# The softmax's division on ScalarE, and other PSUM banks for the first key and value projection, in a hybrid attention and DeltaNet layer

## The chip, the cores and the metric

One NeuronCore of one Trainium2 chip runs the whole kernel. The metric is the device time of one execution in microseconds (us), lower is better. The engines are TensorE (PE; its weight loads are listed apart as PEld), VectorE (DVE), ScalarE (ACT), GpSimd (POOL) and SyncE (SP, which issues most of the loads). Each engine takes its instructions from its own queue in order, so an instruction that waits holds up all that stand behind it in that queue.

## What is computed

One decoder layer, 1024 positions, width 1024, float32:

```
u   = RMSNorm(x);  proj = u @ w_in      # [attn q | k | v | dn q | dn k | dn v | dn z | dn b | dn a]
A   = sliding-window attention (128), 8 query heads, 2 key/value heads, rotary, a sink per head:
        probs = softmax(concat([q k^T * scale + mask, sink]))[..., :-1];  A = probs @ v
B   = gated DeltaNet, 4 heads of 128: conv4 + SiLU, l2 norm, beta, decay, chunks of 64:
        T = (I + L)^-1 per chunk, then a scan over chunks, gated RMSNorm
h   = x + concat(A, B) @ w_o
h  += relu(RMSNorm(h) @ w_up)^2 @ w_down
h  += sigmoid(RMSNorm(h) @ w_gate) * (p @ w_proj);   out = RMSNorm(h)
```

The part that is changed is `probs`: the exponentials of a block of scores, divided by their sum. The other part, the projection `u @ w_in` for the columns of k, v, b and a of the first 512 positions, computes what it did.

## The kernel before

**Matmuls.** Every float32 operand of a projection is split in two fp32r parts, hi and lo, and each product is three passes (hi·hi, hi·lo, lo·hi; `mm3`). A weight slice comes by a load of SyncE into one of two buffers `raw`; ScalarE copies it to hi (L219), VectorE or GpSimd subtracts to get lo (L220), and the pair `w` has four buffers.

**Order.** Generators (`prepare`, `chain`, `attend`, `pairs`, with `projections` as filler) issue the work in a rough interleaving; then the scheduler of the tile framework orders each engine's queue by its own model of durations and readiness. So an edit of one helper moves instructions of other helpers, on every engine, from the edited place until the layer's up projection.

**PSUM.** Eight banks in three rings: g has 3 (the projections), d has 4 (the attention, and the first inverse), e has 1 (small matmuls). `gemm_a` takes its four banks by a string of ring names. The first query projection takes "gggd"; so does the first key/value projection behind it (`CKV`, 96 matmuls of 128x264, weight slices w25, w27, w31 and w35), so that in the kernel before its banks are those that the query projection has to give back by four copies (L478). Its results leave by twelve ScalarE instructions (`kv_evac`, L470 to L472), once the rows' norms are there (`prepare`: `u_rstd`, then `rows_rstd`, which builds `dg` on VectorE and `rsb0` from a matmul over it). The decay scalars (`scalars`, L629 to L652, ending in `gg`) start from `ba`, the last of these results. The first DeltaNet key projection (`CDK`, weight slices w40, w49, w57, w59) follows.

**Attention.** 32 units, each two heads by one block of 128 queries. A unit: four score matmuls into a d bank, masked maximum on VectorE (L549), exponential with its sum on ScalarE, a head at a time (L555), reciprocal of the sums on VectorE (L557), the product of both heads with it (L558), four transposes of `s` on TensorE (L106), a copy to `pt` (L569, VectorE or ScalarE by turns), and the product with v. `s` has three buffers. A unit is two steps behind its scores (`lag`). Filler matmuls of the projections stand between a unit's steps on TensorE.

**DeltaNet.** Per half of 512 positions: convolution (`conv_evac`, L404 to L415), l2 norms, `pre`, an inverse of 31 steps on VectorE alone (L773 to L778), four merges (L800 to L830), then a scan of four pairs of chunks in two head groups (L885 to L958). Filler between these is what is left of `projections`, the embedding product and the output projection `w_out`. The up and down projections and the gate follow.

Of the kernel before, what the change touches and what calls it, by code (L numbers as in the profile page):

```python
# [12 lines left out]
AF = mybir.ActivationFunctionType  # L13
ALU = mybir.AluOpType
# [15 lines left out]
CQ, CKV, CDQ, CDK, CDV, CDZ = 0, 512, 776, 1288, 1800, 2312  # L30
NKV = 264
# [20 lines left out]
class Flow:  # L52
# [11 lines left out]
    def step(self):  # L64
        for x in self.tasks:
            w = x[1]
            if w.done if isinstance(w, (Event, Banks)) else w <= self.now:
                try:
                    w = next(x[0])
                    x[1] = w if isinstance(w, (Event, Banks)) else self.now + w  # L70
                except StopIteration:
                    self.tasks.remove(x)
                return
        if self.filler and (self.hold is None or self.hold.done):
            try:
                self.hold = next(self.filler)
            except StopIteration:
                self.filler = None
            return
        if self.spare:  # L80
            try:
                next(self.spare)
            except StopIteration:
                self.spare = None
            return
        self.now = min(x[1] for x in self.tasks if not isinstance(x[1], (Event, Banks)))
# [23 lines left out]
def bc(ap, dim, n):  # L110

    a = ap.unsqueeze(dim)
    shape = list(a.shape)
    shape[dim] = n
    return a.to_broadcast(shape)
# [3 lines left out]
def hybrid_block(ctx, tc, t, out):  # L119
    nc = tc.nc  # L120
    V, A, G, SY = nc.vector, nc.scalar, nc.gpsimd, nc.sync
# [4 lines left out]
    def nm(s):  # L126
        cnt[0] += 1
        return f"{s}{cnt[0]}"
# [28 lines left out]
    def take(k):  # L157

        live = ring[k]
        while live.n == 0:  # L160
            yield live
        live.n -= 1
        b = bank(ps[k])

        def free():
            live.n += 1
        return b, free
# [54 lines left out]
    def wunit(src, n=512, lo_eng=None, sp=None, raw=None):  # L222
        if raw is None:
            raw = wraw.tile([P, WN], F32, tag="raw", name=nm("raw"))
        SY.dma_start(raw[:, :n], src)
        w = (sp or wsp).tile([P, 2, 512 if sp else WN], F32R, tag="w", name=nm("w"))
        split(w[:, 0, :n], w[:, 1, :n], raw[:, :n], lo_eng or G)
        return w[:, :, :n]
# [3 lines left out]
    def mm3(o, lh, rh, first, last, **k):  # L232
        for i, (a, b) in enumerate(PASSES):
            T.matmul(o, lh(a), rh(b), start=first and i == 0, stop=last and i == 2, **k)
# [9 lines left out]
    def uview(u, b, kt):  # L244
        o = (b * KT + kt) * HB
        return u[:, o:o + HB]

    def gemm_a(c0, u, evac, names, n=512, lo_eng=None, step=None, done=None, after=None, raws=None):

        bs = []  # L250
        for k in names:
            bs.append((yield from take(k)))
        for kt in range(KT):
            if step:
                step(kt)
            if 2 * n > WN:
                w, o = wunit(t["w_in"][kt * P:(kt + 1) * P, c0:c0 + n], n, lo_eng, raw=raws and raws(kt)), 0
            elif kt % 2 == 0:
                w, o = wunit2(t["w_in"], kt // 2, c0, lo_eng, n), 0
            else:  # L260
                o = n
            for m in range(4):
                mm3(bs[m][0][:, :n], lambda a: uview(u, a, kt)[:, m * P:(m + 1) * P],
                    lambda b: w[:, b, o:o + n], kt == 0, kt == KT - 1)
                yield
        if done:
            done.done = True
        if after:
            yield after
        for m in range(4):  # L270
            evac(m, bs[m][0])
            bs[m][1]()
# [121 lines left out]
    def rs(tt):  # L394
        return rstd[:, tt:tt + 1]
# [47 lines left out]
    U0 = up0.__enter__().tile([P, 8192], F32R, tag="U0", name="U0")  # L443
# [22 lines left out]
    def kv_evac(hb):  # L466
        def evac(m, b):
            tt = hb * 4 + m
            kraw[tt] = scr[:, 1024 + m * P:1024 + (m + 1) * P]
            A.activation(kraw[tt], b[:, 0:P], AF.Copy, scale=rs(tt))  # L470
            A.activation(vA[:, tt], b[:, P:2 * P], AF.Copy, scale=rs(tt))
            A.activation(ba[:, tt], b[:, 2 * P:NKV], AF.Copy, scale=rs(tt))  # L472
        return evac
# [59 lines left out]
    def att_scores(n, gp, kv, qT):  # L533

        lo = 0 if n else P
        h0 = kv * 4 + gp * 2
        st = lambda x: atp.tile([P, 2], F32, tag=x, name=nm(x), bufs=4)
        b, free = yield from take("d")
        mx, sm = st("mx"), st("sm")
        s = atp.tile([P, 2, 257], F32, tag="s", name=nm("s"), bufs=3)  # L540
        G.tensor_copy(s[:, :, 256], sinkB[:, h0:h0 + 2])
        b = b.rearrange("p (g s) -> p g s", g=2)
        j = slice(n % 4 + lo // P, n % 4 + 2)
        for i in range(2):
            o = b[:, i, lo:256].rearrange("p (j s) -> p j s", s=P)
            T.matmul(o, qT[:, kv, gp * 2 + i], kH[:, kv, j], start=True, stop=False)
            T.matmul(o, qT[:, kv, gp * 2 + i], kL[:, kv, j], start=False, stop=True)
        for i in range(2):
            V.tensor_tensor_reduce(  # L549
                out=s[:, i, lo:256], in0=b[:, i, lo:256], in1=amask[:, lo:256],  # L550
                scale=1.0, scalar=NEG, op0=ALU.add, op1=ALU.max, accum_out=mx[:, i:i + 1])
        free()
        V.scalar_tensor_tensor(mx, mx, -1.0, nsink[:, h0:h0 + 2], op0=ALU.mult, op1=ALU.min)  # L553
        for i in range(2):
            A.activation(s[:, i, lo:257], s[:, i, lo:257], AF.Exp, bias=mx[:, i:i + 1],  # L555
                         accum_out=sm[:, i:i + 1])
        V.reciprocal(sm, sm)  # L557
        V.tensor_tensor(s[:, :, lo:256], s[:, :, lo:256], bc(sm, 2, 256 - lo), op=ALU.mult)  # L558
        return s

    def att_pt(n, kv, s):
# [521 lines left out]
    def projections():  # L1083
        yield from gemm_a(CQ, U0, lambda m, b: aq_evac(0)(m, slice(None), b), "gggd", lo_eng=V,
                          step=u_step(0, U0, G), done=x_done[0],
                          raws=lambda kt: H[:, kt * 512:kt * 512 + 512])
        yield from gemm_a(CKV, U0, kv_evac(0), "gggd", n=NKV, lo_eng=V,
                          after=rstd_done[0])
        kv_done[0].done = True
        yield from gemm_b2(CDK, U0, conv_evac(1, 0, k0, cvp), V, mm3)  # L1090
        yield from gemm_a2(t["w_in"], CQ, U1, aq_evac(1), lo_eng=G, step=u_step(1, U1, G),
                           done=x_done[1])
        yield rope_done[0]
        yield from gemm_a(CKV, U1, kv_evac(1), "gggd", n=NKV, lo_eng=V,
                          after=rstd_done[1])
        kv_done[1].done = True
        yield from gemm_b2(CDQ, U0, conv_evac(0, 0, q0, cvp), V, mm3)
        dk_done[0].done = True
        yield from gemm_b2(CDV, U0, conv_evac(2, 0, v0, cvp), V, mm3h)
        yield rope_done[1]  # L1100
        yield from gemm_a2(t["w_in"], CDZ, U0, z_evac(0), G)
        up0.__exit__(None, None, None)
        dl = px.enter_context(tc.tile_pool(name="dl", bufs=1))
        k1, q1, v1 = X1 = [dt_([P, 4, HB + 3], f"x{i}1", dl) for i in "kqv"]
        x1.extend(X1)
        z_done[0].done = True
        yield from gemm_b2(CDK, U1, conv_evac(1, 1, k1, cvp), G, mm3h)
        yield from gemm_b2(CDQ, U1, conv_evac(0, 1, q1, cvp), G, mm3h)
        dk_done[1].done = True
        yield from gemm_b2(CDV, U1, conv_evac(2, 1, v1, cvp), V, mm3h)  # L1110
        yield opened
        yield from gemm_a2(t["w_in"], CDZ, U1, z1_evac, G)
        mix_split(0, 0)
        z_done[1].done = True
        flow.spare = embed()
        yield pairs_done[0]
        rest, flow.spare = flow.spare, None
        for _ in rest or ():
            yield
        mix_split(0, 4)  # L1120
        dn1.extend(h4(part(x, F32R)) for x in ("AT0", "Z"))
        mixed.done = True
        yield from w_out(0)
        mix_split(1, 0)
        yield from w_out(1)
# [353 lines left out]
    for kt in range(KT):  # L1479
        for nh in range(2):  # L1480
            i = kt * 2 + nh
# [5 lines left out]
            hi, lo = m[:, o:o + 512], m[:, o + 512:o + 1024]  # L1487
# [5 lines left out]
    for tt in range(NT):  # L1493
# [5 lines left out]
        for q in range(2):  # L1499
            hi, lo = (nT[:, i, q * 4:q * 4 + 4] for i in range(2))  # L1500
# [102 lines left out]
```

## Time and profile before

| | |
|---|---|
| median of 3 runs | 1368.83 us (1366.04 to 1369.57) |
| the profiled execution | 1368.76 us, of which its span, first to last instruction, 1367.0 |
| mean granted TensorE clock | 0.988 |
| busy in the span | PE 1324.5 us, DVE 850.1, ACT 549.8, POOL 436.1 |
| TensorE idle | 42.5 us, in many pieces |

The profile is of one execution. A busy time is a sum over an engine's instructions; an idle time in front of an instruction is put down to the event that released it last. The granted clock is the share of the full rate (2.4 GHz) that TensorE had in a stretch. The first score matmuls start at 76 us and VectorE's last copy to `pt` at 273; the first inverse from 269 to 322, the second from 433 to 469, the last scan ends at about 553; from there to the end the up and down projections and the gate run.

### The profile page before, as it was taken

What the parts mean: (1) busy time and instruction counts of PE and PEld (TensorE: products, weight loads), DVE (VectorE), ACT (ScalarE), POOL (GpSimd) and SP (SyncE); (2) the same over time, 40 slices, a digit from 0 to 9 for tenths busy, and PEclk for the clock granted to TensorE, in tenths of its full rate; (3) what the DMA queues carried; (4) which work ended last, traced back from release to release, by engine and by line L of the source; (5) the groups of instructions that cost most, each with busy time, mean ns of one, the idle gap of its engine ahead of it and who ended that gap; (6) DMA issues with size and microseconds to landing.
All of it is one profiled execution on the core that took longest, in us unless ns stands there. A gap on an engine that the chain in (4) does not pass through costs nothing.

```text
span 1367.0 us, 20403 instructions
## 1 busy us (share of the span) xinstructions
PE 1324.5 (97%) x7664; PEld 1123.5 (82%) x7664; DVE 850.1 (62%) x1566; ACT 549.8 (40%) x1082; POOL 436.1 (32%) x428
## 2 busy tenths in 40 slices
PE   8989999999999999989999999999999999999997
PEld 7778778999888999976788888877888888888886
DVE  6786968698567755697766766656443333344553
ACT  7455466544444434573333333334121212221333
POOL 6673626632375543200011111103222212210332
PEclk9999999999999999899999999999999999999999
DMA  6322222233135431321343333346333323222211
GB/s 220 90 54 76 58 55 52 66 78 99 42 119 168 135 106 47 108 84 56 111 151 123 99 102 116 117 145 222 110 114 103 91 65 123 77 93 71 76 62 47
DMA packets 102738, 134.33 MB, mean 98 GB/s; under 512 B 16400, under 2 KB 71744, under 8 KB 102384
## 3 DMA queue, kind: packets, MB, share of 16 engines
q1 hardware_dynamic: 90528, 110.50, 26.9%
q10 hardware_dynamic: 11760, 21.77, 4.5%
q8 instruction: 60, 0.98, 0.3%
q0 software_dynamic: 352, 0.76, 0.2%
q14 instruction: 38, 0.31, 0.1%
HBM read 106.77 MB, written 26.23 MB: 97 GB/s over the span
## 4 chain that ended last, share of the span: by engine, by line
PE 64%; DVE 5%; DMA 2%; ACT 2%; issue 1%; POOL 1%; SPq 0%; POOLq 0%; DVEq 0%; ACTq 0%
PE bk L102 63%; PE bk L106 1%; DMA PD<-po 1%; DMA raw<-in_w_up 1%; DVE w L220 1%; DMA raw<-in_w_proj 0%; DMA raw<-in_w_down 0%; ACT w L219 0%; DMA rD<-LD 0%; DVE R L1277 0%; DVE T L220 0%; ACT T L1276 0%; DVE rB L1245 0%; DVE S L1358 0%; DVE t L1301 0%
## 5 line engine op out<-in xcount | busy, mean ns | idle before, releaser
L102 PE MATMUL bk<-T,w 128*128 128x512 f32 x2304 | 537.7, 392 | 6.5 <-DVE t L1363 5.2
L102 PEld LDWEIGHTS bk<-T,w 128*128 128x128 f32 x2304 | 433.3, 188 | 102.6 <-DVE t L1363 5.7
L220 POOL TENSOR_TENSOR w<-raw,w 128x512 fp32r<-128x512 f32 x136 | 181.8, 1339 | 622.5 <-ACT w L219 603.7
L219 ACT CAST w<-raw 128x512 fp32r<-128x512 f32 (+1 forms) x280 | 173.1, 621 | 454.8 <-PE bk L102 334.6
L102 PE MATMUL bk<-R,w 128*128 128x256 f32 (+1 forms) x1536 | 243.6, 313 | 2.8 <-ACT po L1070 2.1
L102 PEld LDWEIGHTS bk<-R,w 128*128 128x128 f32 x1536 | 211.6, 189 | 24.8 <-issue 2.3
L220 DVE TENSOR_TENSOR w<-raw,w 128x512 fp32r<-128x512 f32 (+1 forms) x144 | 107.8, 749 | 64.5 <-ACT w L219 64.3
L1475 DVE TENSOR_TENSOR H<-bk,H 128x512 f32<-128x512 f32 x96 | 64.7, 690 | 96.1 <-PE bk L102 96.1
L102 PE MATMUL bk<-U,w 128*128 128x512 f32 (+1 forms) x384 | 77.3, 349 | 1.0 <-ACT ba L472 0.6
L102 PEld LDWEIGHTS bk<-U,w 128*128 128x128 f32 x384 | 59.4, 192 | 17.4 <-issue 7.3
L102 PE MATMUL bk<-w,U 128*128 128x256 f32 (+2 forms) x384 | 65.0, 322 | 4.7 <-ACT AT L478 2.3
L102 PE MATMUL bk<-AT,w 128*128 128x256 f32 (+1 forms) x256 | 66.5, 348 | 2.7 <-ACT w L219 2.2
L102 PE MATMUL bk<-w,R 128*128 128x256 f32 (+1 forms) x480 | 66.8, 288 | 0.1
L102 PEld LDWEIGHTS bk<-w,R 128*128 128x128 f32 x480 | 59.8, 188 | 7.6 <-issue 6.1
L102 PEld LDWEIGHTS bk<-w,U 128*128 128x128 f32 x384 | 55.9, 195 | 11.5 <-ACT AT L478 2.5
L1348 ACT ACTIVATE t<-t 128x512 f32<-128x512 f32 x64 | 40.5, 632 | 49.8 <-DVE t L1347 44.4
L102 PEld LDWEIGHTS bk<-AT,w 128*128 128x128 f32 x256 | 43.8, 197 | 9.8 <-ACT w L219 3.1
L220 POOL TENSOR_TENSOR T<-ra,T 128x1024 fp32r<-128x1024 f32 x14 | 33.7, 2404 | 47.1 <-ACT T L219 44.7
L102 PE MATMUL bk<-R,T 128*128 128x512 f32 (+1 forms) x204 | 48.7, 386 | 0.0
L102 PE MATMUL bk<-T,T 128*128 128x512 f32 (+1 forms) x204 | 47.0, 379 | 0.0
L555 ACT ACTIVATE s<-s,mx 128x257 f32<-128x257 f32 (+1 forms) x64 | 31.3, 491 | 36.6 <-DVE mx L553 32.6
L102 PEld LDWEIGHTS bk<-T,T 128*128 128x128 f32 x204 | 36.8, 188 | 7.8
(370 smaller groups left out, 1893.5 us busy)
## 6 DMA issues: line engine op xcount, KB each, us to landing
raw<-in_w_in SPq DMA_DIRECT2D x72, 256.0 KB, 2.8
raw<-in_w_up SPq DMA_DIRECT2D x32, 512.0 KB, 4.9
AD<-t ACTq DMA_DIRECT2D x64, 256.0 KB, 2.8
raw<-in_w_down SPq DMA_DIRECT2D x64, 256.0 KB, 2.9
ra<-AD SPq DMA_DIRECT2D x28, 512.0 KB, 4.2
raw<-in_w_o SPq DMA_DIRECT2D x32, 256.0 KB, 3.0
PD<-po SPq DMA_DIRECT2D x16, 256.0 KB, 3.0
rawg<-in_w_gate SPq DMA_DIRECT2D x16, 256.0 KB, 3.2
```

What stands on the lines that cost most here:

```text
L102: self.tc.nc.tensor.matmul(o, lh, rh, **k)
L106: self.tc.nc.tensor.transpose(o, x, i)
L219: A.copy(hi, src)
L220: lo_eng.tensor_tensor(lo, src, hi.bitcast(F32), op=ALU.subtract)
L555: A.activation(s[:, i, lo:257], s[:, i, lo:257], AF.Exp, bias=mx[:, i:i + 1], accum_out=sm[:, i:i + 1])
L1348: A.activation(r, r, AF.Square)
L1475: V.tensor_tensor(h, bs[m], h, op=ALU.add)
```

## The change

```
--- before
+++ after
166.00:170.00 4.00, 4.00 (x20) 0.57 0.36 89 att_scores
         V.reciprocal(sm, sm)
-        V.tensor_tensor(s[:, :, lo:256], s[:, :, lo:256], bc(sm, 2, 256 - lo), op=ALU.mult)
+        for i in range(2):
+            A.activation(s[:, i, lo:256], s[:, i, lo:256], AF.Copy, scale=sm[:, i:i + 1])
         return s
166.00:170.00 4.00, 4.00 (x20) 0.57 0.36 89 projections
-        yield from gemm_a(CKV, U0, kv_evac(0), "gggd", n=NKV, lo_eng=V,
+        yield from gemm_a(CKV, U0, kv_evac(0), "dddg", n=NKV, lo_eng=V,
                           after=rstd_done[0])
```

Per unit one VectorE product over both heads (128 by 2 x 256; 128 by 2 x 128 in the four units of the first block, which has no block before it) becomes two ScalarE copies, each with a column of reciprocals as its scale. The first key/value projection takes three d banks that nothing has used yet and one g bank. Line numbers grow by one behind L558: the new copies are L559, `kv_evac` and what stands ahead keep theirs, and the inverse is L774 to L779. From the up projection on all queues read alike in both kernels.

ScalarE's queue at the end of the first key/value projection, before against after. `rh32` is the split of the rows' norms, w35 the projection's last weight slice, w40, w49 and w57 slices of the DeltaNet key projection, `bk20` the first of the projection's four banks.

```order
 L353 ACTIVATE R1_75<-AT13_78,gmix_85 128x512 x2
-L219 CAST rh32_401<-rstd_102 128x4
 L356 ACTIVATE AT13_78<-AT13_78 128x512
 L353 ACTIVATE R1_75<-AT13_78,gmix_85 128x512
+L356 ACTIVATE AT13_78<-AT13_78 128x512 x2
+L219 CAST rh32_401<-rstd_102 128x4
 L219 CAST w35_430<-raw34_428 128x528
-L356 ACTIVATE AT13_78<-AT13_78 128x512 x2
 L219 CAST w40_477<-raw39_475 128x512
 L219 CAST w49_530<-raw48_528 128x512
+L391 COPY rsb0_129<-bk36_457 128x512
+L219 CAST w57_570<-raw56_568 128x512
```

The split of the norms has moved behind three squares, and the copy of `rsb0` and the cast of w57, which stood behind the twelve evacuations (L470 to L472), now stand directly ahead of them.

ScalarE's queue at the first normalized unit, s86, before against after; `H_76` is the Silu of the first convolution, s90 and s96 are the next two units.

```order
 L555 ACTIVATE s86_781,sm85_780<-s86_781,mx84_779 128x129 x2
-L219 CAST kH_131<-bk69_662 128x2x128
-L219 CAST w125_1066<-raw124_1064 128x512
 L415 ACT_TABLE_LOAD
 L415 ACTIVATE H_76<-H_76 128x4x512
+L219 CAST w125_1071<-raw124_1069 128x512
+L219 CAST kH_131<-bk69_662 128x2x128
 L555 ACT_TABLE_LOAD
-L555 ACTIVATE s90_814,sm89_813<-s90_814,mx88_812 128x129 x2
+L555 ACTIVATE s90_815,sm89_814<-s90_815,mx88_813 128x129
+L559 ACTIVATE s86_781<-s86_781,sm85_780 128x128 x2
```

The division of s86 stands behind the Silu, two table loads and the first exponential of s90; before, it was on VectorE and stood behind none of them.

TensorE's queue in front of the first merge of the DeltaNet's first half; `R1_75` with w is filler of the projections, XT and ka belong to the merge. Before:

```order
L102 MATMUL bk607_4067<-R1_75,w641_4247 128x256 x6
L102 MATMUL bk606_4066<-R1_75,w641_4247 128x256 x6
L102 MATMUL bk607_4067<-R1_75,w641_4247 128x256 x6
L102 MATMUL bk606_4066<-R1_75,w657_4336 128x256 x3
L102 MATMUL bk523_3478<-XT0521_3474,ka314_2249 64x64 x8
```

After:

```order
L102 MATMUL bk606_4098<-R1_75,w657_4368 128x256 x6
L102 MATMUL bk607_4099<-R1_75,w657_4368 128x256 x6
L102 MATMUL bk668_4451<-w671_4455,R1_75 128x256 x12
L102 MATMUL bk668_4451<-w677_4504,R1_75 128x256 x9
L102 MATMUL bk669_4452<-w671_4455,R1_75 128x256 x12
L102 MATMUL bk669_4452<-w677_4504,R1_75 128x256 x6
L102 MATMUL bk668_4451<-w677_4504,R1_75 128x256 x3
L102 MATMUL bk669_4452<-w677_4504,R1_75 128x256 x6
L102 MATMUL bk668_4451<-w691_4589,R1_75 128x256 x6
L102 MATMUL bk669_4452<-w691_4589,R1_75 128x256 x6
L102 MATMUL bk668_4451<-w691_4589,R1_75 128x256
L102 MATMUL bk523_3510<-XT0521_3506,ka314_2269 64x64 x8
```

The slice w657 is used up ahead of the merge instead of behind its start, and 61 matmuls of the next projection (`bk668`, `bk669`) stand ahead of it as well.

## Rows read from the trace of the kernel before

**Rows 1.** The page's busy times: engine, us, share of the span, instructions.

```profile
PE 1324.5 (97%) x7664; PEld 1123.5 (82%) x7664; DVE 850.1 (62%) x1566; ACT 549.8 (40%) x1082; POOL 436.1 (32%) x428
```

**Rows 2.** What TensorE waited for: us in total, times, longest us.

```profile
PE bk L106 <- DVE s L558: 4.5, 2, 3.4
...
PE bk L106 <- DVE oS L947: 3.4, 2, 2.5
...
PE bk L102 <- ACT AT L478: 2.3, 1, 2.3
PE bk L102 <- DVE w L220: 1.9, 3, 1.5
PE bk L102 <- DVE pt L569: 1.7, 1, 1.7
```

**Rows 3.** VectorE by line and shape, 80 to 290 us: busy us, mean ns.

```profile
L558 DVE TENSOR_TENSOR s<-s,sm 128x512 f32<-128x512 f32 x28 | 23.2, 829 | 0.6
...
L558 DVE TENSOR_TENSOR s<-s,sm 128x256 f32<-128x256 f32 x4 | 3.0, 751 | 0.1
```

**Rows 4.** ScalarE by line and shape, 80 to 290 us: the nearest shapes.

```profile
L410 ACT ACTIVATE cv<-H,cw 128x512 f32<-128x512 f32 x8 | 5.6, 722 | 2.6 <-DVE H L404 2.6
...
L478 ACT COPY AT<-bk 128x256 f32<-128x256 f32 x8 | 2.5, 378 | 0.0
...
L470 ACT ACTIVATE Z<-bk,rstd 128x128 f32<-128x128 f32 x4 | 1.5, 384 | 1.3 <-PE bk L102 1.3
```

**Rows 5.** TensorE's timeline, first projections: start us, us, work, idle before it.

```profile
33.72 9.40 PE L102 MATMUL bk<-w,U 128*128 128x264 f32 x64 [2.28 <-ACT AT L478]
44.63 3.08 PE L102 MATMUL bk<-w,U 128*128 128x264 f32 x23 [1.51 <-DVE w L220]
...
48.77 11.88 PE L102 MATMUL bk<-U,w 128*128 128x512 f32 x50 [0.59 <-ACT ba L472]
...
63.61 0.39 PE L102 MATMUL bk<-gg,con 128*128 128x16 f32 x2 [0.61 <-DVE gg L648]
```

**Rows 6.** GpSimd's timeline, 33 to 50 us.

```profile
39.86 3.54 POOL L358 TENSOR_TENSOR rsb<-rsb,AT 128x512 f32<-128x512 f32 x2 [1.50 <-ACT AT L356]
```

**Rows 7.** VectorE's timeline, 30 to 66 us.

```profile
43.88 0.70 DVE L220 TENSOR_TENSOR w<-raw,w 128x528 fp32r<-128x528 f32 x1
45.16 1.43 DVE L220 TENSOR_TENSOR w<-raw,w 128x512 fp32r<-128x512 f32 x1 [0.59 <-ACT w L219]
```

**Rows 8.** ScalarE's timeline, 30 to 66 us.

```profile
47.94 0.36 ACT L470 ACTIVATE Z<-bk,rstd 128x128 f32<-128x128 f32 x1
...
51.18 0.63 ACT L219 CAST w<-raw 128x512 fp32r<-128x512 f32 x1 [0.44 <-DMA raw<-in_w_in]
```

**Rows 9.** TensorE's timeline, the first normalized units.

```profile
89.55 0.41 PE L106 MATMUL bk<-con,s 128*128 128x128 f32 x2 [3.44 <-DVE s L558]
...
93.72 0.41 PE L106 MATMUL bk<-con,s 128*128 128x128 f32 x2 [1.02 <-DVE s L558]
```

**Rows 10.** ScalarE's timeline there.

```profile
90.31 1.28 ACT L555 ACT_TABLE_LOAD   x1
91.61 0.41 ACT L555 ACTIVATE s<-s,mx 128x129 f32<-128x129 f32 x1
```

**Rows 11.** TensorE's timeline, a late unit.

```profile
165.50 0.65 PE L102 MATMUL bk<-pt,vA 128*64 128x256 f32 x2 [1.74 <-DVE pt L569]
```

**Rows 12.** A stretch of TensorE alone: its us, PE busy (instructions), granted clock, DMA.

```profile
166.00:170.00 4.00, 4.00 (x20) 0.57 0.36 89
```

**Rows 13.** TensorE's timeline, the first merge.

```profile
317.82 14.06 PE L102 MATMUL bk<-R,w 128*128 128x256 f32 x117
332.69 0.68 PE L102 MATMUL bk<-XT,ka 64*64 64x64 f32 x16 [0.81 <-DVE XT L800]
```

**Rows 14.** All engines, the last scans: busy us of PE, PEld, DVE, ACT, POOL, then PEclk.

```profile
450.00:540.00 90.00, 90.00 (x881) 86.91 (x880) 56.93 (x146) 35.67 (x94) 41.85 (x38) 1.00 0.29 86
540.00:560.00 20.00, 16.55 (x102) 15.27 (x101) 8.71 (x28) 6.35 (x22) 4.74 (x7) 0.74 0.13 41
```

## The prediction

> **What bounds the kernel now.** I read the page's busy times first. TensorE works 1324.5 of 1367.0 us [rows 1]; the reader is to see that VectorE, at 62%, and ScalarE, at 40%, have slack as a whole, so that work taken off one and put on the other is worth only what TensorE waits for it. All its idle time is 1367.0 − 1324.5 = 42.5 us, and no edit of this kind can bring more than that and the stretches at a low clock. Second the list of TensorE's waits, to see which of the 42.5 us has to do with the edited lines [rows 2]: 4.5 us for the product that is removed (L558), 1.7 us for a VectorE copy (`pt`, L569) late in the attention, 2.3 us for the evacuation of the banks that the first key/value projection takes, 1.9 us for lo parts. Third the timelines around each of these waits, since the change reorders queues from there on. A part of the waits (3.4 us on `oS`) is in the scans, far behind the edit, and can only move.
>
> My sum is made against the profiled execution: 1368.76 us, span 1367.0 and 1.76 around it; it is 0.07 below the median of the runs shown, so no correction is made.
>
> **The division itself.** VectorE loses 28 products at 829 ns and 4 at 751 ns [rows 3]: 23.2 + 3.0 = 26.2 us of 850. ScalarE gains 64 scaled copies, 56 of 128x256 and 8 of 128x128. No row has the exact form. From below: a 128x256 copy without a scale column takes 378 ns, a 128x128 one with it 384 ns; from above: a 128x512 one with it 722 ns [rows 4]. I take 0.40 us, next to the two nearest shapes: 64 × 0.40 = 25.6 us (24 to 46 by the bounds), which brings ScalarE to some 575 us of 1367. Both are beside TensorE. For a single unit it is a wash: 2 × 0.40 = 0.80 us against 0.83. What a unit pays beyond that is order: the division now waits in ScalarE's queue for what is ahead of it there, and while it waits for the reciprocal from VectorE, the next unit's exponential and the casts of weight slices stand behind it. Filler matmuls cover that, as they cover it now for 30 of 32 units: only two waits on L558 exist [rows 2]. So the terms are places, not units. Zero for the units as such; from −2 to +4 us.
>
> The Trainium skill, in "ScalarE: Activation LUTs", section "Rules for kernel authors", says that multiplications should go to VectorE rather than ScalarE, and would count this change as a loss; by its section on what a table load costs (186 ns + 0.833 ns per column, 93 ns more per scale column, 93 ns of overlap) a 128x256 copy with a scale column is an estimated 0.40 us. No run here shows that such a copy costs that; the rule weighs the pair against a VectorE faster than this trace's, where the product took 829 ns on average beside a busy GpSimd.
>
> **Place 1, the first key/value projection (28 to 66 us).** The change names three d banks that need no evacuation. I give that nothing: by the order TensorE does 17 instead of 9 of its matmuls before it touches the g bank, but that bank's copy (L478) stands in ScalarE's queue where it stood, so the stall ahead of the 64 matmuls [rows 5], 2.28 us, stays within half a us; it ends when the first L478 does. If the bank came free without it, −2.3. Against that stand the moved rows. GpSimd's power for the norms now stands behind two more additions of the pair's 1.77 us each [rows 6], and the lo part of w35 behind it; I work it out to end near 46.3 instead of 44.58 us (43.88 + 0.70) [rows 7]. The stall of 1.51 us ahead of the last 23 matmuls becomes 3.2, of which four matmuls of the key projection and the `dg` matmul, now ahead, fill about 1.5: +0.2. The wait of 0.59 us for the last evacuation goes, since the key projection has two free g banks: −0.6. But the twelve evacuations now stand behind the cast of w57, which waits for its load: it ran at 51.18 us, released by the load [rows 8]; the load's buffer comes free with the lo part of w40 (46.6 us by [rows 7]), now about half a us later. So the evacuations start near 52 instead of 47.94 us [rows 8]; by the lo parts of weights that VectorE has put behind it instead of in between, I take `gg` to be late by about 3 us of these 4, at 66.3. TensorE reached its matmuls at 63.61 − 0.61 = 63.0; now at 63.0 + 0.2 − 0.6 and five matmuls of 11.88 / 50 = 0.24 us later by the order, 63.8. It stalls 2.5 instead of 0.61 us: +1.9. Sum +0.2 − 0.6 + 1.9 = **+1.5**. If the load lands early, −1.5; if the stall lowers the clock too, +5.
>
> **Place 2, the first normalized units (84 to 98 us).** TensorE waits 3.44 and 1.02 us here, 4.46 together [rows 9]. The first division leaves VectorE, but on ScalarE it stands behind the Silu, the reload of the exponentials' table (to 90.31 + 1.28 = 91.59) and one exponential (to about 92.0) [rows 10], so the first scaled copies end near 92.8, later than the product did, whose reader started at 89.55. TensorE now has 17 more filler matmuls ahead, 17 × 0.12 = 2.0 us [rows 13], and two transposes of keys; it reaches its first transpose of s86 at about 88.5 instead of 89.55 − 3.44 = 86.1. That one needs the first copy alone (92.4): 3.9 us. The second unit is ready soon after, so that a second wait is small, 0.3. 4.2 against 4.46: **−0.3**. At best all goes, −4.5; at worst, with a second wait left, +2.
>
> **Place 3, the copy to `pt` at 163.7 us.** TensorE waits 1.74 us [rows 11] because VectorE has four convolution steps, a product L558 and lo parts ahead of the copy; from 166 to 170 us, behind it, the granted clock is 0.57 [rows 12], which loses 4 × 0.43 = 1.7 us. In the new order the copy stands ahead of the convolution steps and TensorE has 20 matmuls instead of 4 between the transposes and the product with v. Both go: −1.74 − 1.7 = **−3.4**; if VectorE is late for another reason, 0.
>
> **Place 4, the DeltaNet's place in the filler.** The first merge now has 61 more filler matmuls ahead. At 14.06 / 117 = 0.12 us each [rows 13] that is 7.3 us; the wait of 0.81 us for the merge's input [rows 13] goes, and all merges and scans come 7 to 10 us later relative to the projections. Filler used early is missing late: in the last scans some 84 matmuls fewer stand between the steps, 84 × 0.12 = 10 us of cover. Before, the last 20 us already show 3.45 us of idle and a clock of 0.74 [rows 14]. VectorE has 26 us less to do in the attention, but in the new order the convolutions of the second half are inside the inverse's steps, so the inverse's end is not earlier by that. Bounds: −3 (the scans' waits of 3.4 us [rows 2] gone) to +10 (no cover for the missing filler). From 450 to 540 us TensorE is busy for 90.00 of 90 us [rows 14], so these steps had more cover than they needed; I take the value near the lower end, **+1.5**.
>
> **Sum.** 0 + 1.5 − 0.3 − 3.4 + 1.5 = −0.7; 1368.76 − 0.7 = **1368.1 us**.
>
> **Rivals.** (a) *Faster*: VectorE's relief is what counts, and the stalls it caused go: place 2 whole, −4.46, place 3, −3.4, and place 1 without a new stall, 0: 1368.8 − 7.9 = 1360.9. For it: the two waits on L558, with the 1.7 us on `pt`, are all that the attention's VectorE work costs TensorE in [rows 2], and both stand on what VectorE had ahead of them. Against it: the order puts the first copies behind two table loads. (b) *Slower*: the missing filler in the last scans. It decides from the point at which a scan step (matmul, VectorE, ScalarE, GpSimd's power, transposes) takes longer than the filler left beside it; then up to 10 us are exposed, some of it at half clock. With +8 there, +1.5, −0.3 and −3.4: 1374.6. For it: the end of the scan is already exposed [rows 14]. Against: the merges end without a wait before. (c) *The change doesn't do what it says*: the banks change nothing, as the g bank is still waited for; that is in my sum. (d) *The units grow*: by the upper bound the pair on ScalarE takes 2 × 0.72 = 1.44 us [rows 4] against 0.83 [rows 3], 0.6 us more per unit; with the fourth part of 32 units uncovered that is +4.9 on my sum, 1373.0. Against it: 30 of 32 units are covered now. This is the outcome to which the Trainium skill's rule, in the section named above, would lead.
>
> **How the numbers follow.** 0.3% or 4.1 us is about what a measurement can tell from no change. Chances: forecast 0.42, (a) 0.32, (b) 0.20, (d) 0.06. So faster 0.32, within 0.3% 0.42, slower 0.26. The forecast's own range is 1364.7 to 1372.9. For eight in ten I reach past (a) to 1358, most of the way to all best ends (−1.5 − 4.5 − 3.4 − 3), and past (b) to 1377.
>
> **What would show it.** In the new profile: (1) the stall behind the first matmuls of the key/value projection still released by L478, near 2.3 us; (2) `gg` released later than 63.6 us, with more than 2 us of TensorE idle in front of its matmuls; (3) a wait of 4 to 5 us near 88 us released by ScalarE's L559, not by VectorE; (4) no wait on `pt` near 164 us and no low clock there; (5) VectorE near 824 us, ScalarE near 575; (6) the stretch of the last scans with more idle time than 3.45 us, by a little. The forecast is wrong if (3) is gone, or if (6) shows over 6 us, or if a wait on L559 appears at many units.

## The result and the profile after

The change makes the kernel slower: 1378.36 us median of 6 runs (1375.67 to 1381.5) against 1367.03 of 6 (1363.84 to 1369.57), ratio 1.0081 with a 95% interval of 1.0067 to 1.0096. The forecast was 1368.1 and the range ended at 1377. The profiled execution took 1378.0 us with a span of 1376.2, 9.2 more than the one of before.

In the diff under "The change", the two lines that begin with `166.00:170.00` are not code: they show the row of [rows 12], followed by the name of the function that is edited (`att_scores`, `projections`).

The page's busy times of the kernel after, to lay beside [rows 1]:

```profile
PE 1331.2 (97%) x7664; PEld 1125.8 (82%) x7664; DVE 815.3 (59%) x1534; ACT 575.0 (42%) x1146; POOL 432.0 (31%) x428
```

The work has moved as it should: VectorE lost 34.8 us and ScalarE gained 25.2. Of VectorE's 34.8, 26.2 were the removed products; the instruction counts differ by those 32 alone, so the rest is the same instructions taking less time, and why they do was not followed. TensorE's idle time is 1376.2 − 1331.2 = 45.0 us, only 2.5 more than before; the other 6.7 us stand as busy time. A reader who compares idle times alone therefore misses most of the loss. Matmuls that run at the low clock count as busy, but the mean granted clock differs little (0.986 against 0.988); waits too short to show as idle time may make up the rest, which was not measured.

What TensorE waited for in the kernel after (us in total, times, longest), against [rows 2]:

```profile
PE bk L106 <- DVE oS L948: 6.4, 6, 1.7
PE bk L102 <- DVE w L220: 3.8, 4, 1.5
...
PE bk L102 <- ACT AT L478: 2.8, 1, 2.8
PE bk L106 <- DVE kL L220: 2.7, 1, 2.7
...
PE bk L106 <- ACT s L559: 1.1, 1, 1.1
```

The 4.5 us on the product of `s` are gone from VectorE, 1.1 of them have come back on ScalarE's L559, and 2.7 on the keys' lo part beside it. The waits on `oS` in the scans have doubled, from 3.4 in two to 6.4 us in six.

**Where the 9.2 us are.** Both kernels run the same 7664 matmuls in other orders. I gave each matmul the spacing (start to next start) that its shape usually has in the trace of before, added these up along each run's own order, and read when a run reached the same sum. The difference is how late it is at equal work; each profile is compared with the one profile of before. "Filler" is the number of matmuls of the second half's projections (those that read `R`), of the embedding and of the output projection that stand in TensorE's order ahead of the first merge, from there to the second half's first merge, and from there to the last scan product; in most kernels these add up to 1780, in two of them (e5, e7) 23 more stand behind that.

| stretch of before | before 320 us | 320 to 480 | 480 to 572 | to the end |
|---|---|---|---|---|
| filler before | 843 | 645 | 292 | |
| filler after | 925 | 659 | 196 | |
| us lost by after | +2.2 | +1.1 | +6.7 | −0.7 |

The loss is for the most part in the last merges and scans. At the places where both kernels have run exactly the same matmuls, no spacing is needed for this reading: there, after is 2.2 us late at 320 us, 4.0 at 475 and 10.0 at 570, so that 0.7 us of the split between the two later stretches hangs on the method. The same stretch in both kernels (all engines: busy us of PE, PEld, DVE, ACT, POOL, then PEclk), before:

```profile
480.00:570.00 90.00, 86.55 (x804) 82.50 (x803) 51.19 (x124) 37.87 (x103) 34.45 (x32) 0.94 0.28 86
```

after:

```profile
480.00:570.00 90.00, 83.18 (x761) 76.83 (x761) 48.82 (x132) 32.68 (x94) 32.00 (x31) 0.94 0.23 65
```

In the same 90 us TensorE runs 43 matmuls fewer and is idle for 6.8 instead of 3.4 us; the granted clock is 0.94 in both. The two stretches of [rows 14] in after:

```profile
450.00:540.00 90.00, 85.21 (x804) 79.50 (x804) 61.93 (x172) 34.09 (x87) 38.24 (x34) 1.00 0.31 95
540.00:560.00 20.00, 15.91 (x122) 14.67 (x122) 10.09 (x27) 8.59 (x28) 6.47 (x6) 0.92 0.18 53
```

The 90 us without an idle moment are gone: 4.8 us idle between 450 and 540. But 3.5 of these lie ahead of the second half's first merge, which comes at 494 us in after and at 479 in before, so they belong to the middle stretch. From that merge to the last scan product (552 us in before, 564 in after) TensorE is idle for 3.0 us in before and for 6.2 in after.

How the DeltaNet came late. VectorE's timeline at the start and end of the first half's inverse, before:

```profile
268.73 1.21 DVE L773 TENSOR_TENSOR rD<-rD,bS 128x1024 f32<-128x1024 f32 x1
...
322.24 0.18 DVE L778 TENSOR_TENSOR bk<-bk,tp 128x16 f32<-128x16 f32 x1
```

and after:

```profile
270.90 0.69 DVE L750 TENSOR_TENSOR ka<-bk,et 128x512 f32<-128x512 f32 x1 [3.10 <-PE bk L102]
...
275.46 1.28 DVE L774 TENSOR_TENSOR rD<-rD,bS 128x1024 f32<-128x1024 f32 x1 [1.75 <-DMA rD<-LD]
276.66 0.74 DVE L412 SCALAR_TENSOR_TENSOR cv<-xk,cw,cv 128x512 f32<-128x512 f32 x1
277.32 0.17 DVE L778 TENSOR_TENSOR tp<-rD,bk 128x31 f32<-128x31 f32 x1
277.42 1.40 DVE L412 SCALAR_TENSOR_TENSOR cv<-xk,cw,cv 128x512 f32<-128x512 f32 x2
...
335.26 0.18 DVE L779 TENSOR_TENSOR bk<-bk,tp 128x16 f32<-128x16 f32 x1
```

The inverse begins 6.7 us later, since its last input product stands later in TensorE's queue (and its last input is then a load, 1.75 us). It takes 60.0 instead of 53.7 us: convolution steps (L412) stand between its own in both kernels, 30 of them (26.9 us) instead of 24 (20.8 us). TensorE's timeline at the first merge, against [rows 13]:

```profile
336.38 7.41 PE L102 MATMUL bk<-w,R 128*128 128x256 f32 x61
343.72 0.68 PE L102 MATMUL bk<-XT,ka 64*64 64x64 f32 x16
```

There is no stall here: the 61 added matmuls fill the time, and are missing later.

### The profile page after: what moved, and what is told of

Its sections match the earlier page's. It is cut to its first block, busy times and chain, and to the rows that moved or that the text cites. A ratio compares the mean times of both kernels' runs of the same rounds, so it can differ in the third digit from the quotient of the medians.

```text
span 1376.2 us, 20434 instructions
## 1 busy us (share of the span) xinstructions
PE 1331.2 (97%) x7664; PEld 1125.8 (82%) x7664; DVE 815.3 (59%) x1534; ACT 575.0 (42%) x1146; POOL 432.0 (31%) x428
## 4 chain that ended last, share of the span: by engine, by line
PE 76%; DVE 9%; DMA 6%; ACT 3%; issue 3%; POOL 2%; SPq 1%; POOLq 0%; ACTq 0%; DVEq 0%
PE bk L102 74%; PE bk L106 2%; DMA raw<-in_w_o 1%; DVE w L220 1%; ACT w L219 1%; DMA raw<-in_w_up 1%; DMA AD<-t 1%; DMA raw<-in_w_down 1%; DMA raw<-in_w_in 1%; DMA H<-in_w_in 1%; POOL rsb L358 1%; POOL w L220 1%; DMA AT<-in_xT 0%; DVE cv L412 0%; DVE gg L646 0%
## 5 line engine op out<-in xcount | busy, mean ns | idle before, releaser
L102 PEld LDWEIGHTS bk<-R,T 128*128 128x128 f32 x204 | 36.2, 188 | 7.4
```

Source lines behind the costliest of these rows:

```text
L102: self.tc.nc.tensor.matmul(o, lh, rh, **k)
```

## The experiments

Theory A: the banks cost some 2 us early; the division of the later query blocks makes the DeltaNet late against its filler, and the last merges and scans lose their cover. Rivals: B, the loss starts with the banks; C, only both parts together lose; D, every unit pays for its ScalarE copies; E, the copies and not the position cost the time. All kernels compute everything. In each job the runs are compared with those of before on the same chip.

**e1, banks only:** before with

```
-        yield from gemm_a(CKV, U0, kv_evac(0), "gggd", n=NKV, lo_eng=V,
+        yield from gemm_a(CKV, U0, kv_evac(0), "dddg", n=NKV, lo_eng=V,
```

> Only the PSUM banks of the first key/value projection are changed; the division stays on VectorE. TensorE's order is that of after up to the first score matmuls and that of before from there on. Theory A (the loss comes from the division, which moves the DeltaNet later against its filler): +1.5 to +3 us against before, all of it before 75 us, ratio 1.001 to 1.002. Theory B (the loss starts with the banks and is carried on): +8 us or more, ratio 1.006. Theory C (the two parts only lose together): within 0.1% of before.

Measured: 1.0016 (1.0007 to 1.0025), 1366.86 against 1364.10 us. As A; B falls.

**e2, division only:** after with `"gggd"` as in before.

> Only the division is moved to ScalarE; banks as before. The first merge stands 9 us of TensorE work later than in before, the last scans have less filler. Theory A: +6 to +9 us (about +1.5 at the first normalized units, -3 at the copy to pt near 164 us, +8 from 380 us to the end of the last scan), ratio 1.005 to 1.0065. Theory B: within 0.2% of before. Theory C: within 0.1% of before.

Measured: 1.0056 (1.0042 to 1.0070). As A; C falls, the parts add up (0.16% + 0.56% against 0.81%).

**e3, division on ScalarE in query blocks 4 to 7 only:** before with

```
-        V.tensor_tensor(s[:, :, lo:256], s[:, :, lo:256], bc(sm, 2, 256 - lo), op=ALU.mult)
+        if n >= 4:
+            for i in range(2):
+                A.activation(s[:, i, lo:256], s[:, i, lo:256], AF.Copy, scale=sm[:, i:i + 1])
+        else:
+            V.tensor_tensor(s[:, :, lo:256], s[:, :, lo:256], bc(sm, 2, 256 - lo), op=ALU.mult)
```

> Division on ScalarE only in the 16 units of query blocks 4 to 7, on VectorE in blocks 0 to 3; banks as before. The DeltaNet's merges stand where they stand in after (9 to 10 us of TensorE work later than before). Theory A: +8 to +10 us against before, as the loss of the last scans comes without the gain at 164 us. Rival D (each unit pays for the ScalarE copies, so the loss goes with the number of units): about half of the division's loss, +3 to +4 us.

Measured: 1.0086 (1.0072 to 1.0100). Half of the copies cost more than all of them: D falls.

**e4, division on ScalarE in blocks 1 to 3 only:** the same with `if 0 < n < 4:`.

> Division on ScalarE only in the 12 units of query blocks 1 to 3, on VectorE elsewhere; banks as before. The DeltaNet stands where it stands in before. Theory A: no loss in the scans, and VectorE's relief can be seen by itself: -3 us against before if the stall at the copy to pt near 164 us goes, else 0. Rival D: +2 to +3 us.

Measured: 1.0002 (0.9992 to 1.0011). No loss, as A has it, and no gain that can be measured either, though its profile is 2.0 us ahead of before's at 320 us (1.4 of these are before's own profile, see place 3 below).

From the first merge on, TensorE's order in e1 and e4 is that of before, matmul for matmul, and in e3 that of after. So e3 has after's loss with half of its copies, and e4 has none with 12 units on ScalarE.

The next kernels move the DeltaNet's place by the pauses of the rough interleaving. No work is added or taken, but the order of every queue can change from there on.

**e5:** before, and **e6:** after, each with

```
             load_x(s, 1)
-            yield 2.7
+            yield 12.0
```

> Division and banks as before; only the pause with which the merges are issued behind their first loads is 12.0 instead of 2.7 in the rough interleaving. No work is added or taken; the scheduler now puts the second half's merges 10 us of TensorE work earlier, so that 361 filler matmuls instead of 292 stand between the second half's first merge and its last scan product (196 in after). Theory A (time goes as the filler that is left beside the second half's merges and scans): faster than before, by 2 to 6 us, since before has 3.45 us of idle and a low clock at 540 to 560 us. Rival E (the ScalarE copies themselves, not the position, cost the time in e2 and e3): within 0.1% of before.

Measured: 0.9980 (0.9970 to 0.9990), 1361.53 against 1364.48 us. As A; E falls for the position's own part: no copy has been moved.

> All of the change is in, and the same pause is 12.0 instead of 2.7: 287 filler matmuls beside the second half's merges and scans instead of 196. Theory A: the loss of about 8 us goes, so +1 to +4 us against before (what the banks and the first normalized units cost, less the gain at 164 us), ratio 1.001 to 1.003. Rival E: as after, 1.008.

Measured: 0.9992 (0.9980 to 1.0004). The loss of the change is gone with both of its edits in, and a little more than A expected. E falls.

**e7:** e4 with that same pause of 12.0.

> Division on ScalarE in query blocks 1 to 3 only, banks as before, the pause 12.0: 358 filler matmuls beside the second half's merges and scans. Theory A: the gain of e4's copy to pt (its profile was 2 to 3 us ahead of before's) and that of the pause add up: -4 to -8 us against before. Rival E: as e4, no difference.

Measured: 0.9958 (0.9945 to 0.9971), 1358.40 against 1364.48 us. It beats both kernels, by 6 us the one of before. The two parts by themselves (1.0002 in e4, 0.9980 in e5) add up to 0.9982, so that two gains add up here, as expected, is not shown.

**e8, division on ScalarE in block 7 only:** `if n == 7:`.

> Division on ScalarE only in the 4 units of the last query block, banks as before. The first half's merges stand where they do in before, the second half's 6 us of TensorE work later, with 235 filler matmuls beside them instead of 292. Theory A: a loss between that of e4 (292) and e3 (196), +3 to +6 us against before, ratio 1.002 to 1.0045. Rival E, and rival D with it (4 of 32 units): within 0.1% of before.

Measured: 1.0120 (1.0107 to 1.0133): a loss, as against D and E, but of 16 us where A has 3 to 6. The stretch of A's loss has +4.2 us (table below). More is lost ahead of it, where a cast of a weight slice waits for its load in this order; TensorE's timeline in e8:

```profile
455.92 0.99 PE L102 MATMUL bk<-R,w 128*128 128x256 f32 x4 [4.81 <-ACT w L219]
```

and ScalarE's:

```profile
455.25 0.62 ACT L219 CAST w<-raw 128x512 fp32r<-128x512 f32 x1 [5.58 <-DMA raw<-in_w_o]
```

A does not speak of such a stall. It is not of this order alone: e5 and e7 have one of 4.33 and 3.60 us near 425 us, behind a cast that waits for its load in the same way.

**e9:** before with the pause of e5 at 0.1. **e10:** before with the pause ahead of the second half's norms

```
-        yield 5.5
+        yield 12.0 if hb else 5.5
```

> The kernel before with the pause ahead of the merges at 0.1 instead of 2.7: division on VectorE, banks as before, no work added. 172 filler matmuls stand beside the second half's merges and scans instead of 292. Theory A: slower than before by 6 to 11 us, ratio 1.0045 to 1.008, lost between 440 and 570 us. Rival E (the ScalarE copies, not the position): within 0.1% of before.

Measured: 0.9995 (0.9983 to 1.0007). **A fails here** as a rule on the whole time. The number is the one that E has, but e6, as fast as before with every copy on ScalarE, and e10, slower with none, rule E out.

> The kernel before with the pause ahead of the second half's norms at 12.0 instead of 5.5: 220 filler matmuls beside the second half's merges and scans. Theory A: slower than before by 3 to 7 us, ratio 1.002 to 1.005. Rival E: within 0.1%.

Measured: 1.0045 (1.0027 to 1.0062), as A, against E. Its profiled run took 1368.89 us, no more than the one of before (1368.76), so its table row shows less of a loss than its runs.

**e11:** e6 with 0.5 for that pause of the second half. **e12:** e4 with the same 0.5.

> All of the change is in; the pause ahead of the merges is 12.0 and that ahead of the second half's norms 0.5: 343 filler matmuls beside the second half's merges and scans, against 196 in after and 287 in e6. Theory A: -1 to -5 us against before, ratio 0.9965 to 0.9995. If the gain of e6 had another cause than the filler: as e6 or slower.

Measured: 1.0026 (1.0013 to 1.0038). Better than after, but slower than before and than e6: A's number fails, and what came is the outcome that the expectation names for another cause of e6's gain than the filler of the last stretch. That stretch does gain here (4.8 us, table below); the loss is ahead of it. Its middle stretch, with 518 filler matmuls, has a stall that no other kernel's trace has there:

```profile
392.61 0.33 PE L106 MATMUL bk<-con,oS 128*128 128x128 f32 x1 [4.13 <-DVE oS L948]
```

> Division on ScalarE in query blocks 1 to 3, banks as before, the pause ahead of the second half's norms 0.5: 344 filler matmuls. Theory A: as e7 (358), -4 to -8 us against before, ratio 0.994 to 0.997.

Measured: 0.9971 (0.9961 to 0.9982), as A, though at the lower gain end.

**What e9 and e11 correct.** The lateness of each profile at equal work, by stretch, sorted by the filler of the last one (us, minus is gained against the profile of before; that profile's 1368.76 us is 4 to 5 us above the medians of before in the experiments, so that the sums of a row lie lower than its ratio; e1 and e4, with before's order from the first merge on, show how much of that is in each column: −2.2 and −1.0 in the middle one, 0.0 in the last):

| kernel | filler: ahead, middle, last | to 320 us | 320 to 480 | 480 to 572 | ratio of the runs |
|---|---|---|---|---|---|
| e9 | 843, 765, 172 | −0.7 | −7.8 | +4.0 | 0.9995 |
| after | 925, 659, 196 | +2.2 | +1.1 | +6.7 | 1.0081 |
| e3 | 925, 659, 196 | +0.5 | +0.3 | +6.7 | 1.0086 |
| e10 | 843, 717, 220 | +0.3 | −0.9 | +1.7 | 1.0045 |
| e2 | 925, 629, 226 | −1.6 | −1.5 | +5.0 | 1.0056 |
| e8 | 836, 709, 235 | −0.8 | +6.8 | +4.2 | 1.0120 |
| e6 | 919, 574, 287 | +2.6 | −4.5 | −4.0 | 0.9992 |
| e1 | 843, 645, 292 | +1.2 | −2.2 | 0.0 | 1.0016 |
| e4 | 843, 645, 292 | −2.0 | −1.0 | 0.0 | 1.0002 |
| e11 | 919, 518, 343 | +2.4 | +1.5 | −4.8 | 1.0026 |
| e12 | 843, 593, 344 | −2.4 | +0.5 | −5.7 | 0.9971 |
| e7 | 838, 561, 358 | −1.9 | +3.1 | −9.3 | 0.9958 |
| e5 | 838, 558, 361 | +0.4 | +4.1 | −9.2 | 0.9980 |

In the last stretch the kernels fall into three groups: under 240 filler matmuls every kernel loses (1.7 to 6.7 us), at 287 to 292 none does, above 340 all gain 4.8 to 9.3 us. TensorE's idle time from the second half's first merge to the last scan product has the same groups, with less scatter: 5.8 to 6.2 us, 2.1 to 3.0, and 0.7 to 1.8. Within a group the count does not order the losses, and much of the scatter is the clock: by half the time at 1.2 GHz, the low clock cost 5.1 us of this stretch in before, after, e1, e3 and e4, 6.8 in e9, 3.4 in e2 and e8, 1.7 in e10, e11 and e12, and nothing in e5, e6 and e7. So e6's 4.0 us, and about half of what e5 and e7 gain, stand as clock. The stretch in e5 (as above, before and after):

```profile
480.00:570.00 90.00, 89.31 (x821) 86.53 (x820) 63.99 (x131) 41.57 (x108) 36.27 (x33) 1.00 0.29 92
```

and in e9:

```profile
480.00:570.00 90.00, 83.74 (x785) 79.07 (x784) 51.90 (x130) 37.04 (x101) 30.72 (x29) 0.92 0.26 80
```

So A holds for its stretch, e9 included. But the filler is a budget. In e9 the 120 matmuls that the last stretch lacks are in the middle one, whose scans wait in before too, and up to 7.8 us come back there (1 to 2 of them are before's own profile, by e1 and e4). In after and e3, 82 of the missing 96 went ahead of the first merge and 14 into the middle; ahead of the merge, the kernel before has few waits that they could fill (0.81 us at the merge, [rows 13]). This is how I read the difference between a loss of 0.8% and none; no run tests it by itself. The middle stretch follows the count less well: e6 gains 4.5 us with a count near that of e7, which loses 3.1, and e5, e7, e8 and e11 have their stalls there (3.6 to 4.8 us each). The rest of the middle stretch was not settled, nor was what in the scheduler's model puts the filler ahead; that the division of the blocks 4 to 7 does it is shown by e3 against e4.

## Why the prediction was wrong

By its own terms, at equal work against the profile of before:

| term | predicted | measured in after |
|---|---|---|
| place 1, key/value projection | +1.5 | +2.1 (at 66 us) |
| place 2, first normalized units | −0.3 | +1.7 (75 to 98 us) |
| place 3, the copy to `pt` | −3.4 | −3.1 (160 to 172 us) |
| place 4, the DeltaNet's place | +1.5 | +7.8 (320 to 572 us) |

**The division itself: right in its place.** One row of ScalarE, 80 to 296 us (busy us, mean ns):

```profile
L559 ACT ACTIVATE s<-s,sm 128x256 f32<-128x256 f32 x56 | 25.4, 502 | 4.2 <-DVE sm L557 4.2
```

One copy takes 502 ns rather than 0.40 us, but two in a row take 0.91 us, since the second starts before the first ends; ScalarE's busy time grew by 25.2 us, foreseen as 25.6. Only one of 32 units made TensorE wait (1.1 us). The estimate from the Trainium skill ("ScalarE: Activation LUTs", "What ACT_TABLE_LOAD costs") is 492 ns for a copy by itself and 0.40 us with the overlap, and the trace agrees with both (502 ns; the second of a pair starts 0.91 − 0.50 = 0.41 us after the first). The Trainium skill's rule on the same page ("Rules for kernel authors"), that a multiplication belongs on VectorE, is not borne out here: the pair takes 0.91 us against the product's 0.83, but e4 has 12 of the units on ScalarE and loses nothing.

**Place 1: right in size, only in part by the steps foreseen.** TensorE's timeline after, against [rows 5]:

```profile
33.76 2.70 PE L102 MATMUL bk<-w,U 128*128 128x264 f32 x13 [2.79 <-ACT AT L478]
...
58.45 4.45 PE L102 MATMUL bk<-U,w 128*128 128x512 f32 x18 [0.78 <-DVE w L220]
64.38 1.67 PE L102 MATMUL bk<-U,w 128*128 128x512 f32 x6 [1.47 <-DVE w L220]
67.13 0.49 PE L102 MATMUL bk<-U,w 128*128 128x512 f32 x1 [1.08 <-DVE w L220]
```

and ScalarE's, against [rows 8]:

```profile
51.44 0.62 ACT L219 CAST w<-raw 128x512 fp32r<-128x512 f32 x1
51.96 0.37 ACT L470 ACTIVATE Z<-bk,rstd 128x128 f32<-128x128 f32 x1
```

The bank that was named away is still waited for, the evacuations start at 51.96 (foreseen near 52) behind the cast of w57, and the scalars are late. But TensorE does not stall on `gg`: it stalls on the lo parts of weights (0.78, 1.47 and 1.08 us) that share VectorE's queue with the scalars. Nor was the clock in the sum: from 28 to 45 us it is 0.80, against 0.90 in before, an estimated 17 × 0.10 = 1.7 us. In e6, where it is 1.00 there, TensorE's order is the same and it is 3.1 us late at 66 us all the same. So the size was right (e1 has this loss by itself, 0.16%), but not the way to it.

**Place 2: the wait right, the clock missed.** TensorE's timeline, against [rows 9]:

```profile
93.67 0.41 PE L106 MATMUL bk<-con,Z 128*128 128x128 f32 x2 [2.75 <-DVE kL L220]
95.22 0.33 PE L106 MATMUL bk<-con,s 128*128 128x128 f32 x1 [1.14 <-ACT s L559]
```

2.75 + 1.14 = 3.9 us against the 4.2 foreseen; the first part is put on the keys' lo part, whose cast stood behind the same Silu. But behind it the granted clock fell, which it did not do in the profile of before, where 3.44 us of idle time stood. The stretch in after:

```profile
97.00:101.00 4.00, 4.00 (x22) 0.71 0.02 4
```

4 × 0.29 = 1.2 of the 1.7 us. This is not a matter of the kernel alone. e9 and e10 have before's order here and the same stall (3.42 us); TensorE's stretch behind it, in before, e9 and e10:

```profile
90.00:95.00 5.00, 3.98 (x31) 1.00 0.21 52
90.00:95.00 5.00, 5.00 (x30) 0.69 0.19 52
90.00:95.00 5.00, 5.00 (x25) 0.50 0.20 52
```

By this e9 lost 0.2 us and e10 1.3 between 75 and 98 us. In e6 and e11, with after's order here, the clock fell as it did in after (0.58 and 0.71 from 97 to 101 us). So of the 1.7 us, 0.2 to 1.3 are what the profile of before was spared. And e2, with the same division and no low clock here, is as late at 160 us as at 75.

**Place 3: the wait right, the clock by luck.** The wait for `pt` fell from 1.74 [rows 11] to 0.31 us:

```profile
167.47 0.65 PE L102 MATMUL bk<-pt,vA 128*64 128x256 f32 x2 [0.31 <-DVE pt L570]
```

and from 166 to 172 us the trace has no low clock. But the low clock of [rows 12] is in the profile of before alone. In e9, with before's order here, TensorE's wait and the stretch behind it are:

```profile
165.67 0.65 PE L102 MATMUL bk<-pt,vA 128*64 128x256 f32 x2 [1.28 <-DVE pt L569]
...
166.00:170.00 4.00, 3.63 (x24) 1.00 0.37 82
```

e9 and e10, which change nothing ahead of the first merge, are 1.4 us ahead here of the profile of before. So of the 3.1 us some 1.7 are the change's, and the forecast's −1.7 for the clock priced an event of one execution.

**Place 4: the step that failed.** The mechanism was named, with rival (b), and its size was taken wrongly: +1.5 forecast, +7.8 measured. The prediction counted 84 matmuls and 10 us of cover that would be missing (96 are), and then took +1.5 "near the lower end", because TensorE was busy for 90.00 of 90 us from 450 to 540 us [rows 14]. It read a fully busy stretch as slack. The runs show that the filler was needed: with 96 fewer the stretch from 480 to 572 us lost 6.7 us, two thirds of what 84 × 0.12 would give, and with the same order e3 lost as much. At 0.12 us for each filler matmul, about half of the loss came up to the scan product that before starts at 540.6 us and after at 551.5, with only 1.2 us of idle time; the other half came behind it, at the end that [rows 14] already shows exposed. So both the busy stretch and the exposed end were priced too low.

Rival (b), at a chance of 0.20, is what came: it had +8 here and 1374.6 us, and the profile has +7.8 from 320 us on. Of the signs named, (6) shows it, with 6.2 us of idle time instead of 3.0 from the second half's first merge to the last scan product. With all four as measured the sum is 2.1 + 1.7 − 3.1 + 7.8 = 8.5, against 9.2 in the spans; the rest is in small pieces between them and behind. The range ended 1.4 us below the measured median.

The gain of rival (a) did not come: of the 7.9 us it counted, 3.1 came, at `pt`, and 1.4 of these belong to the one profile of before.

## What to carry to other kernels

A stretch in which the bound engine is 100% busy is not a stretch with slack: ask how much of that work is filler that could have stood anywhere, and what the dependent steps beside it take without it. Where a scheduler orders the queues, count the filler beside each exposed chain in the order of both kernels before any stall is priced; here the one count (292 to 196) told more than four stalls worked out to a tenth of a microsecond. It does not give the whole time: ask also where the moved filler goes (e9) and what new stall the order brings (e8, e11). Before a stretch at a low clock is priced, see whether a second execution of the same order has it too. And a relief of a busy engine can be had without such a loss: the same division in blocks 1 to 3, with the merges issued later, is 0.42% faster than before (e7; the later merges alone give 0.20%, e5).

## What the runs showed of the hardware

- A copy on ScalarE with a column of scales: 502 ns for 128x256 by itself, 0.91 us for two in a row, 391 ns for 128x128.
- Idle time did not tell the loss: 9.2 us of span, of which 2.5 us are idle time of TensorE, at nearly the same mean granted clock (0.988 and 0.986).
- Whether the clock fell behind a stall differed between executions of the same order: behind 3.42 to 3.44 us of idle time it stayed at 1.00 in before and was 0.69 in e9 and 0.50 in e10 from 90 to 95 us; 2.75 and 1.14 us in after were followed by a stretch at 0.71.
